# Query heads 0 and 1 projected as a column pair, keys normalised together, attention in twelve steps a group with the compressed branch inside

## The chip, the cores and the metric

One Trainium2 chip, of which the kernel uses one core. The metric is the device time of one launch, in microseconds (us); less is better. The engines are named as in the profile: PE (TensorE, matrix products; PEld is its weight load), DVE (VectorE), ACT (ScalarE), POOL (GpSimd), SP (SyncE, which issues the large loads).

## The reference, cut to what matters

One block over 256 tokens of width 4096: a normalised input is multiplied by `w_in`, parts of the product go to an mLSTM branch and to an attention branch with 16 heads in 4 groups, both are gated, and two more 4096-wide products follow (`w_out`, `ple_gate`). All is in float32. The change touches the projections of queries and the attention branch:

```
u = rmsnorm(x) @ w_in          # split: ..., ns_q (2048), ns_kc, ns_vc, ns_ks, ns_vs, ns_kw, ns_vw, ...
q = rmsnorm(ns_q per head)     # 4 groups of 4 heads, head width 128
p_c = softmax(q @ kcmp + bias) # 15 compressed keys of a group
o_c = p_c @ vcmp
o_s = softmax(q @ ks + bias) @ vs   # "selected" branch; with 256 tokens all blocks are chosen
o_w = softmax(q @ kw + bias) @ vw   # window branch, 256 keys, causal
o   = g0 * o_c + g1 * o_s + g2 * o_w
```

## The kernel before, in words

Every large product is made in three passes over a split of both sides into a rounded float32r part and its remainder (`whi`, `wlo` for weights; `sh`, `sl` for activations), and the products of a 128 x 128 block with 512 columns are the unit of PE's work. Weights are streamed in tiles of two 128-row blocks by 512 columns (`raw`, six buffers). A **unit** of the main loop takes one such tile: it issues the split of the tile three units ahead (`whi` on ACT, then `wlo` on DVE, four buffers each), then the 12 products of its own tile, and then one step from each of three queues of background generators (`urgent`, `fifo`, `third`). All engines run the instructions of this one written order, each in its own queue. An instruction waits for what it reads and for the buffer that it writes; what stands behind it on its engine waits too.

Columns of `w_in` are taken in **wide groups** (one 512-column stretch, 16 units, 192 products) or in **pair groups** (`pair_group`, two stretches at once, with a plan in `PLANS` that names 16 row blocks `kp`). In a pair group a row block is either plain (`C`, 24 products) or mixed (`a`/`c`, 7 sub-products of 3 passes, 21 products, with extra sums of weights on DVE, `sums`). The accumulators of a pair group lie in PSUM as `own` and `oth`: one set in the four `mm` banks, the other in the four `sd` banks (`side(i)`, one buffer each), by `bset`.

The attention of a query group is a generator (`t_nq`). It normalises the queries, transposes them, splits them into `qh` and `ql`, makes the compressed branch (scores of 15 keys, softmax, weights, a transpose, in steps of their own), and then walks over eight score tiles (one head, 128 queries of half t): `scores` into `sd0` (PE), `bias_max` (DVE), `expo` (ACT), `coef` (DVE), `scale` (ACT, one unit later), `trans` into `sd1` (PE), `copy_pt` (DVE), `pv` (PE). A tile of t = 0 has 256 columns (two branches of 128 keys), one of t = 1 has 512. A new step is one turn of the main loop, so a step's PE work stands behind 12 large products.

Lines of the kernel before that are named below: L869, L871 (products of wide groups), L1135 (products of pair groups), L1416 and L1417 (`whi`, `wlo`), L475 (compressed scores), L484 to L488 (their bias, maximum, difference), L490 (their exponential), L493 to L500 (their weights), L505 (copies of `vcmp`), L523 (first pass of scores), L534, L536 (bias, maximum), L541 (exponentials), L547 (second half of `coef`), L558 (transposes of weights), L563 (their copy), L1112 (sums of `own` at the end of an early pair group).

Of the kernel before, what the change touches and what calls it, by code (L numbers as in the profile page):

```python
# [63 lines left out]
PLANS = {g: FULL for g in (-4, -3, -2, 1, 2)}  # L64
PLANS[-5] = SIX
PLANS[-9] = PLANS[-7] = SIX
PLANS[-8] = _plan((0, 1, 2, 3, 4, 5), (7, 9, 11, 13), (6, 8, 10, 12), (14, 15))
# [16 lines left out]
def hymba_block(ctx: ExitStack, tc: tile.TileContext, a, out: bass.AP):  # L84
# [40 lines left out]
    pad = sm_.tile([128, 16], F32, name="pad")  # L125
# [29 lines left out]
    rt = cp.tile([128, 2], F32, name="rt")  # L155
    cw = cp.tile([128, 3], F32, name="cw")
# [49 lines left out]
    def t_rms():  # L206
# [11 lines left out]
        yield  # L218
        rsqrt(rt, ss, D)
# [23 lines left out]
    def evac_u(ps, flag):  # L243
        u = utile([128, 2, 512])
        scaled(u[:, 0], ps[0], 0, True)
        scaled(u[:, 1], ps[1], 1, False)
        done.add(flag)
        return u

    def transposed(u, t):  # L250
        p = side(t, [128, 4, 128])
# [50 lines left out]
    def t_small(st):  # L302
        while "own-9" not in done:
            yield
# [49 lines left out]
    def normed(u):  # L354

        sq = sqtile([128, 8, 128])
        v = u.rearrange("p t (h d) -> p (t h) d", d=128)
        nc.scalar.activation(sq, v, AF.Square)
        yield
        ss = small([128, 8], "ss8")  # L360
        nc.vector.tensor_reduce(ss, sq, axis=AX.X, op=OP.add)
        yield
        nc.scalar.activation(ss, ss, AF.Sqrt, scale=1.0 / HD, bias=epst)
        yield
        nc.vector.reciprocal(ss, ss)
        nc.vector.tensor_tensor(v, v, ss[:, :, None].to_broadcast([128, 8, 128]), op=OP.mult)
        yield

    def t_k(u, br):
        if br == 0:  # L370
            for i, n in enumerate(("kh", "kl")):
                held[n] = wk.tile([128, 4, 2, 256], F32R, tag=f"nat{i}", name=n)
        kh, kl = held["kh"], held["kl"]
        yield from normed(u)
        pp = [transposed(u, 0), transposed(u, 1)]
        yield
        c = cw[:, br + 1:br + 2]
        for t in range(2):
            r = slice(t * 128, (t + 1) * 128)
            nc.scalar.activation(kh[:, :, br, r], pp[t], AF.Copy, scale=c)  # L380
            nc.vector.scalar_tensor_tensor(kl[:, :, br, r], pp[t], c, kh[:, :, br, r], op0=OP.mult, op1=OP.subtract)
        yield
# [9 lines left out]
    def t_cmp2():  # L392
        hs = held["hs"]
        hp = wk.tile([128, 2, 4, 128], F32, tag="qt", name="hp", bufs=2)
        nc.gpsimd.memset(hp, 0.0)
        yield
        pp = [side(2, [128, 2, 60]), side(3, [128, 2, 60])]
# [7 lines left out]
        for h in range(4):  # L405
            for c in range(2):
                nc.vector.tensor_copy(hp[:, c, :, 32 * h:32 * h + NCMP],
                                      pp[1][:, c, :].rearrange("p (g b) -> p g b", b=NCMP))
            if h % 2:
                yield  # L410
# [9 lines left out]
        kn = stile([60, 128])  # L420
        nc.scalar.activation(kn, pk, AF.Square, accum_out=ss[0:60])
        nc.scalar.activation(vcmp, pv, AF.Copy)
        yield
        rsqrt(ss[0:60], ss[0:60], HD)
        kn = stile([60, 128])
        nc.scalar.activation(kn, pk, AF.Copy, scale=ss[0:60, 0:1])
        yield
        p = side(3, [128, 60])
        nc.tensor.transpose(p, kn, idn[0:60, 0:60])
# [7 lines left out]
    def t_evac(ps, flag):  # L437
        held[flag] = evac_u(ps, flag)
        unread.append(flag)
        yield  # L440

    def t_nq(flag, g):

        u = held.pop(flag)
        yield from normed(u)
# [9 lines left out]
        yield  # L455
# [10 lines left out]
        for h in range(2):  # L466
            load_tb(h)
        yield
        while "cmp" not in done:
            yield  # L470

        pc = side(0, [128, 8, NCMP])
        for t in range(2):
            for h in range(4):
                MM(pc[:, 4 * t + h, :], qt[:, h, t * 128:(t + 1) * 128], kct[:, g, :], start=True, stop=True)  # L475
        yield

        bd = sqtile([128, 4, 128])
        nc.gpsimd.memset(bd, 0.0)
        sc = small([128, 8, 32], "sc", 1)  # L480
        nc.gpsimd.memset(sc, 0.0)
        scv = sc[:, :, 0:NCMP]
        for t in range(2):
            nc.vector.tensor_tensor(scv[:, 4 * t:4 * t + 4], pc[:, 4 * t:4 * t + 4],  # L484
                                    biasc[:, 8 - 8 * t:23 - 8 * t, 4 * g:4 * g + 4].rearrange("p c h -> p h c"), op=OP.add)
        m8 = small([128, 8], "mx8")
        nc.vector.tensor_reduce(m8, scv, axis=AX.X, op=OP.max)
        nc.vector.tensor_tensor(scv, scv, m8[:, :, None].to_broadcast([128, 8, NCMP]), op=OP.subtract)  # L488
        yield
        nc.scalar.activation(scv, scv, AF.Exp)  # L490
        yield
# [1081 lines left out]
```

## Time and profile before

| | us |
|---|---|
| median of 3 runs | 2117.85 (2117.15 to 2119.14) |
| profiled execution | 2118.3 |
| its span, first to last instruction | 2116.5 |
| PE busy in the span | 2107.0 |
| DVE busy | 1679.7 |
| ACT busy | 1198.6 |
| POOL busy | 30.3 |

The profiled execution took 2118.3 us, of which the traced instructions span 2116.5. TensorE's granted clock is at its full level in all of the span. Products are pipelined: a 128x512 one is shown with 390 ns, but the next starts earlier, so the cost of one is read from starts and counts, not from its own length.

### The profile page before, as it was taken

Reading aid. Unit: us, or ns where it says so; the run is one execution under the profiler, and the core shown is the slowest. Engines: PE = TensorE matmul, PEld = TensorE weight load, DVE = VectorE, ACT = ScalarE, POOL = GpSimd, SP = SyncE. Lnnn points to the kernel's source line nnn. Section 1 sums busy time; section 2 is a strip of 40 time slices with the busy share of each in tenths; the row PEclk is TensorE's granted clock in tenths of the full one; section 3 lists DMA queues with packets and bytes.
Section 4 is the critical chain, followed back from the end, with each engine's and each line's share of the span. In section 5 each row is a group of like instructions: output and inputs, shape, how many; then the busy total and the mean of one; then the engine's idle time right before and its main releaser. Section 6 shows DMA issues by size and latency. Waiting matters only on the chain.

```text
span 2116.5 us, 26925 instructions
## 1 busy us (share of the span) xinstructions
PE 2107.0 (100%) x9696; PEld 1739.3 (82%) x9696; DVE 1679.7 (79%) x2130; ACT 1198.6 (57%) x1545; POOL 30.3 (1%) x69
## 2 busy tenths in 40 slices
PE   9999999999999999999999999999999999999998
PEld 7888788888888888888888888888888888888887
DVE  6697588666656675859989999988898987888988
ACT  6656455555556555456555565666555555555554
POOL 1000000000000000000000000000000000000000
PEclk9999999999999999999999999999999999999999
DMA  9656866654455455646666667565666665666664
GB/s 354 211 185 206 285 203 216 195 167 159 145 174 159 151 177 168 196 145 200 200 206 209 192 207 229 182 213 180 224 211 216 229 221 169 204 201 224 203 218 145
DMA packets 118374, 422.08 MB, mean 199 GB/s; under 512 B 13714, under 2 KB 14026, under 8 KB 118240
## 3 DMA queue, kind: packets, MB, share of 16 engines
q1 hardware_dynamic: 115568, 413.45, 60.4%
q0 software_dynamic: 2528, 6.89, 1.1%
q8 instruction: 76, 1.25, 0.2%
q14 instruction: 58, 0.48, 0.1%
q10 hardware_dynamic: 144, 0.02, 0.0%
HBM read 416.08 MB, written 4.23 MB: 199 GB/s over the span
## 4 chain that ended last, share of the span: by engine, by line
PE 99%; DMA 0%; DVE 0%; ACT 0%; SPq 0%; issue 0%
PE mm L1135 34%; PE sd L1135 33%; PE mm L869 16%; PE mm L871 8%; PE sd L569 1%; PE sd L976 1%; PE sd L558 1%; PE sd L253 0%; PE sd L773 0%; PE sd L582 0%; PE sd L475 0%; DMA raw<-in_w_in 0%; PE sd L525 0%; PE sd L524 0%; PE sd L523 0%; PE mm L956 0%
## 5 line engine op out<-in xcount | busy, mean ns | idle before, releaser
L1416 ACT ACTIVATE whi<-raw 128x1024 fp32r<-128x1024 f32 x839 | 885.1, 1060 | 732.5 <-PE mm L869 133.8
L1417 DVE TENSOR_TENSOR wlo<-raw,whi 128x1024 fp32r<-128x1024 f32 x839 | 1021.9, 1222 | 343.1 <-ACT whi L1416 327.1
L1135 PE MATMUL sd<-whi,sh 128*128 128x512 f32 x852 | 276.1, 390 | 0.0
L1135 PE MATMUL sd<-wlo,sh 128*128 128x512 f32 x852 | 275.7, 389 | 0.0
L1135 PE MATMUL sd<-whi,sl 128*128 128x512 f32 x852 | 275.6, 389 | 0.0
L1135 PE MATMUL mm<-whi,sh 128*128 128x512 f32 x840 | 272.9, 393 | 0.3 <-ACT mv L200 0.3
L1135 PE MATMUL mm<-whi,sl 128*128 128x512 f32 x840 | 270.0, 389 | 0.0
L1135 PE MATMUL mm<-wlo,sh 128*128 128x512 f32 x840 | 269.9, 389 | 0.0
L869 PE MATMUL mm<-whi,sh 128*128 128x512 f32 x768 | 245.1, 400 | 1.4 <-ACT whi L1416 1.4
L869 PE MATMUL mm<-whi,sl 128*128 128x512 f32 x768 | 237.4, 390 | 0.0
L871 PE MATMUL mm<-wlo,sh 128*128 128x512 f32 x768 | 237.1, 390 | 0.0
L1135 PEld LDWEIGHTS sd<-wlo,sh 128*128 128x128 f32 x852 | 159.9, 188 | 33.2
L1135 PEld LDWEIGHTS sd<-whi,sl 128*128 128x128 f32 x852 | 159.9, 188 | 33.2
L1135 PEld LDWEIGHTS sd<-whi,sh 128*128 128x128 f32 x852 | 159.6, 188 | 33.3 <-issue 0.4
L1135 PEld LDWEIGHTS mm<-whi,sl 128*128 128x128 f32 x840 | 157.7, 188 | 33.1
L1135 PEld LDWEIGHTS mm<-wlo,sh 128*128 128x128 f32 x840 | 157.6, 188 | 33.1 <-DVE wlo L1417 0.2
L1135 PEld LDWEIGHTS mm<-whi,sh 128*128 128x128 f32 x840 | 155.8, 188 | 34.4 <-issue 2.7
L871 PEld LDWEIGHTS mm<-wlo,sh 128*128 128x128 f32 x768 | 144.0, 188 | 31.6 <-DVE wlo L1417 0.8
L869 PEld LDWEIGHTS mm<-whi,sl 128*128 128x128 f32 x768 | 144.2, 188 | 31.0
L869 PEld LDWEIGHTS mm<-whi,sh 128*128 128x128 f32 x768 | 139.6, 189 | 29.1 <-issue 1.9
L1135 PE MATMUL mm<-whi,cb 128*128 128x512 f32 x416 | 134.6, 389 | 0.0
L1135 PE MATMUL sd<-whi,cb 128*128 128x512 f32 x352 | 117.5, 389 | 0.0
(315 smaller groups left out, 1875.2 us busy)
## 6 DMA issues: line engine op xcount, KB each, us to landing
raw<-in_w_gate SPq DMA_DIRECT2D x192, 512.0 KB, 3.6
raw<-in_w_in SPq DMA_DIRECT2D x191, 512.0 KB, 3.5
raw<-in_w_out SPq DMA_DIRECT2D x128, 512.0 KB, 4.0
raw<-in_ple_gate SPq DMA_DIRECT2D x128, 512.0 KB, 3.5
raw<-in_w_early SPq DMA_DIRECT2D x96, 512.0 KB, 3.9
raw<-in_w SPq DMA_DIRECT2D x16, 512.0 KB, 4.3
u<-in_xt SPq DMA_DIRECT2D x16, 256.0 KB, 7.7
xn<-in_x SPq DMA_DIRECT2D x4, 1024.0 KB, 7.1
```

The lines of the kernel that those rows point to most:

```text
L558: nc.tensor.transpose(psd[i][:, b, s, :], sb[i][:, b, s * 128:(s + 1) * 128], idn)
L569: MM(o[t][:, h, :], ptb[i][:, b, s, :], v[:, s, b, g * 128:(g + 1) * 128], start=False, stop=(i == 6 + t and b == 1 and s == t))
L869: MM(box["ps"][t], s[c][:, k, t * 128:(t + 1) * 128], m[:, j, :], start=st, stop=False)
L871: MM(box["ps"][t], sh[c][:, k, t * 128:(t + 1) * 128], lo[:, j, :], start=False, stop=last)
L976: MM(o[64 * kv:64 * kv + 60], xq[l // 8][:, l % 8, 60 * kv:60 * kv + 60], raw[:, j, 256 * kv:256 * kv + 256], start=(l == 0), stop=(l == 31))
L1135: MM(acc.t, s, m, start=acc.i == 0, stop=acc.i == acc.n - 1)
L1416: nc.scalar.activation(hi, r, AF.Copy)
L1417: nc.vector.tensor_sub(lo, r, hi)
```

## The change

The query stretches nq0 and nq1 leave the wide groups and become a pair group, -7, with five mixed row blocks; the early pair groups before it move up by one number (-10, -9, -8). Group -5 takes the plan FULL (seven mixed) in place of SIX. The two key branches are normalised and transposed in one generator (`t_keys`). Queries are no longer scaled before their norm (the epsilon is scaled instead, `epsr`). The normalisation of a query group is a generator of its own in the third queue (`t_query`). In `t_nq` two tiles of t = 0 are joined (four 128-key blocks, 512 columns), so that there are six score tiles, the compressed branch's work is distributed over the first five steps of the tile loop, and `pv` follows a tile four steps later, not three.

```diff
-EARLY = {-9: ("vs", "vw"), -8: ("mv0", "mv1"), -7: ("ks", "kw")}
-ORDER = ["kc", "vc", "small", -9, -8, -7,
-         "nq0", "nq1", "nq2", "nq3", "mq0", "mk0", "mq1", "mk1", "mv2", "mv3"]
+EARLY = {-10: ("vs", "vw"), -9: ("mv0", "mv1"), -8: ("ks", "kw"), -7: ("nq0", "nq1")}
+ORDER = ["kc", "vc", "small", -10, -9, -8, -7,
+         "nq2", "nq3", "mq0", "mk0", "mq1", "mk1", "mv2", "mv3"]
...
-PLANS = {g: FULL for g in (-4, -3, -2, 1, 2)}
-PLANS[-5] = SIX
+PLANS = {g: FULL for g in (-5, -4, -3, -2, 1, 2)}
+PLANS[-7] = _plan((0, 1, 2, 4), (3, 5, 7, 9, 11), (6, 8, 10, 12, 13), (14, 15))
...
+        def cmp_weights():
+            sm = small([128, 8], "sm8")
+            nc.vector.tensor_reduce(sm, scv, axis=AX.X, op=OP.add)
+            nc.vector.reciprocal(sm, sm)
...
+        tiles = [((0, 1), 0), ((0,), 1), ((1,), 1), ((2, 3), 0), ((2,), 1), ((3,), 1)]
...
-        for i in range(11):
+        for i in range(10):
 
             at(scores, i)
+            if i == 0:
+                cmp_scores()
             at(trans, i - 2)
-            if i == 2:
-                for t in range(2):
-                    MM(o[t].rearrange("p h d -> p (h d)"), pct[:, t, :], bd.rearrange("p h d -> p (h d)"),
-                       start=True, stop=False)
-            at(pv, i - 3)
+            if i == 3:
+                cmp_trans()
+            if i == 4:
+                cmp_values()
+            at(pv, i - 4)
             at(bias_max, i)
             at(copy_pt, i - 2)
             at(expo, i)
             at(coef, i)
-            if i < 8:
+            if i < 4:
+                (cmp_max, cmp_exp, cmp_weights, cmp_copy)[i]()
+            if i < 6:
                 behind.append(lambda i=i: scale(i))
             yield
...
-        bset = g % 2
+        bset = (g + (g < -6)) % 2
...
-                evq.extend(("oth-7", "oth-7"))
+                evq.extend(("own-7", "own-7"))
```

Three places in the orders of the engines' queues matter. The first is DVE's queue in the first query group, at the third score tile. Of the kernel before, from one split to the next (`wlo` is the split of a weight tile, `s` the scores with their bias, `mx` their maximum, `pt` the copy of transposed weights, `sm` the sums of exponentials):

```order
L1417 TENSOR_TENSOR wlo_3913<-raw_3735,whi_3912 128x1024
L534 TENSOR_TENSOR s_3943<-sd0_3932,tb_3675 128x512
L536 TENSOR_REDUCE mx2_3945<-s_3943 128x2
L563 COPY pt_3947<-sd1_3936 128x512
L546 RECIPROCAL sm2_3949<-sm2_3949 128x2
L547 TENSOR_TENSOR sm2_3949<-sm2_3949,sg_118 128x2
L1417 TENSOR_TENSOR wlo_3955<-raw_3754,whi_3954 128x1024
```

Of the changed kernel, DVE's queue from one split to the next at step 2 (`sc` holds the compressed scores, `sm8` their sums):

```order
L1471 TENSOR_TENSOR wlo_4172<-raw_3982,whi_4171 128x1024
L570 TENSOR_TENSOR s_4200<-sd0_4191,tb_4073 128x512
L573 TENSOR_REDUCE mx_4202<-s_4200 128x2
L604 COPY pt_4204<-sd1_4195 128x512
L586 RECIPROCAL sm_4206<-sm_4206 128x2
L588 TENSOR_TENSOR sm_4206<-sm_4206,sg_119 128x2
L520 TENSOR_REDUCE sm8_4211<-sc_4095 128x8
L521 RECIPROCAL sm8_4211<-sm8_4211 128x8
L522 TENSOR_TENSOR sm8_4211<-sm8_4211,sg_119 128x8
L524 TENSOR_TENSOR sc_4095<-sc_4095,sm8_4211 128x8x15
L526 TENSOR_TENSOR sc_4095<-sc_4095,mask01_c_101 128x4x15 x2
L1471 TENSOR_TENSOR wlo_4223<-raw_4002,whi_4222 128x1024
```

The weights of the compressed branch (L520 to L526), which before stood between two splits with no score tile beside them, now stand behind a score tile's `coef`. On ACT, at steps 1 and 2 of the changed kernel, the exponential of the compressed scores (L516) and the four copies of `vcmp` (L530) stand between the tile's exponentials and the next `whi`:

```order
L581 ACTIVATE s_4157,sm_4163<-s_4157,mx_4159 128x256 x2
L516 ACTIVATE sc_4095<-sc_4095 128x8x15
L1470 ACTIVATE whi_4171<-raw_3982 128x1024
L592 ACTIVATE s_4157<-s_4157,sm_4163 128x256 x2
L581 ACTIVATE s_4200,sm_4206<-s_4200,mx_4202 128x256 x2
L530 ACTIVATE sq_4168<-vcmp_121 32x128 x4
L1470 ACTIVATE whi_4222<-raw_4002 128x1024
```

In the kernel before these two pieces stood between two `whi` with no tile's exponentials between. The second place is PE's queue at step 3 of the changed kernel, from the last large product of the unit to the first of the next (`sd0` takes the scores, `sd1` the transposes of tile 1, `sd2` the transposes of the compressed weights `sc`):

```order
L916 MATMUL mm1_3884<-wlo_4078,sh6_427 128x512
L560 MATMUL sd0_4242<-k_3299,qh_4062 128x256
L561 MATMUL sd0_4242<-k_3299,ql_4063 128x256
L562 MATMUL sd0_4242<-k_3300,qh_4062 128x256
L560 MATMUL sd0_4242<-k_3299,qh_4062 128x256
L561 MATMUL sd0_4242<-k_3299,ql_4063 128x256
L562 MATMUL sd0_4242<-k_3300,qh_4062 128x256
L599 MATMUL sd1_4249<-idn_81,s_4157 128x128 x4
L535 MATMUL sd2_4254<-idn_81,sc_4095 128x128 x2
L914 MATMUL mm0_3883<-whi_4131,sh6_427 128x512
```

And at step 4 (the products with `pct`, the copy of those transposes, open the output banks):

```order
L916 MATMUL mm1_3884<-wlo_4132,sh6_427 128x512
L560 MATMUL sd0_4294<-k_3299,qh_4062 128x512
L561 MATMUL sd0_4294<-k_3299,ql_4063 128x512
L562 MATMUL sd0_4294<-k_3300,qh_4062 128x512
L599 MATMUL sd1_4298<-idn_81,s_4200 128x128 x4
L545 MATMUL sd2_4303<-sq_4168,pct_4096 128x512
L545 MATMUL sd3_4304<-sq_4168,pct_4096 128x512
L611 MATMUL sd2_4303<-vsw_1744,pt_4204 128x128 x4
L914 MATMUL mm0_3883<-whi_4171,sh7_484 128x512
```

Both pieces stood in units without score tiles, or two units after their input, in the kernel before; now each stands one step behind the DVE work that it reads. The third place is the end of pair group -7 of the changed kernel, on PE (`mm0_3163` to `mm1_3166` are the `own` accumulators, `mm0_3883` and `mm1_3884` the first two of the wide group nq2):

```order
L1189 MATMUL mm1_3165<-wlo_3799,sh7_484 128x512
L1189 MATMUL mm1_3166<-wlo_3799,sh7_484 128x512
L914 MATMUL mm0_3883<-whi_3818,sh0_153 128x512
L914 MATMUL mm1_3884<-whi_3818,sh0_153 128x512
L914 MATMUL mm0_3883<-whi_3818,sl0_154 128x512
L914 MATMUL mm1_3884<-whi_3818,sl0_154 128x512
```

and on DVE, where those accumulators are read:

```order
L1158 TENSOR_TENSOR u_3792<-mm0_3163,u_3792 128x512
L1158 TENSOR_TENSOR u_3792<-mm0_3164,u_3792 128x512
L1158 TENSOR_TENSOR u_3793<-mm1_3165,u_3793 128x512
L1158 TENSOR_TENSOR u_3793<-mm1_3166,u_3793 128x512
L1471 TENSOR_TENSOR wlo_3878<-raw_3772,whi_3877 128x1024
```

A name mm0 or mm1 has two buffers, so the first accumulator of nq2 takes the buffer of `mm0_3163` and the second that of `mm1_3165`. In the kernel before, the last early pair group held its `own` accumulators in the `sd` banks, and the wide group behind it began in `mm` banks.

## Rows read from the trace of the kernel before

**Rows 1.** The page, part 4: shares of the chain that ended last.

```profile
PE 99%; DMA 0%; DVE 0%; ACT 0%; SPq 0%; issue 0%
```

**Rows 2.** Busy time by engine (us, instructions) in a stretch of gate pair groups.

```profile
1025.00:1100.00 75.00, 75.00 (x332) 62.10 (x331) 67.62 (x75) 42.69 (x47) 0.00 (x0) 1.00 0.63 202
```

**Rows 3.** Timeline, DVE, first query group: start, us, engine, line, out<-in [idle before].

```profile
463.94 0.42 DVE L534 TENSOR_TENSOR s<-sd,tb 128x256 f32<-128x256 f32 x1 [1.08 <-PE sd L525]
464.40 0.42 DVE L536 TENSOR_REDUCE mx<-s 128x2 f32<-128x256 f32 x1
...
467.87 0.69 DVE L534 TENSOR_TENSOR s<-sd,tb 128x512 f32<-128x512 f32 x1
468.59 0.69 DVE L536 TENSOR_REDUCE mx<-s 128x2 f32<-128x512 f32 x1
...
470.63 0.16 DVE L547 TENSOR_TENSOR sm<-sm,sg 128x2 f32<-128x2 f32 x1
471.38 1.23 DVE L1417 TENSOR_TENSOR wlo<-raw,whi 128x1024 fp32r<-128x1024 f32 x1 [0.59 <-ACT whi L1416]
472.52 0.42 DVE L534 TENSOR_TENSOR s<-sd,tb 128x256 f32<-128x256 f32 x1
```

**Rows 4.** Timeline, ACT, the same stretch.

```profile
464.86 0.40 ACT L541 ACTIVATE s<-s,mx 128x128 f32<-128x128 f32 x1 [3.59 <-DVE mx L536]
...
465.65 1.04 ACT L1416 ACTIVATE whi<-raw 128x1024 fp32r<-128x1024 f32 x1
...
469.31 0.51 ACT L541 ACTIVATE s<-s,mx 128x256 f32<-128x256 f32 x1 [2.03 <-DVE mx L536]
...
470.31 1.04 ACT L1416 ACTIVATE whi<-raw 128x1024 fp32r<-128x1024 f32 x1
```

**Rows 5.** Timeline, all engines, two score tiles before the group's last.

```profile
495.14 0.69 DVE L536 TENSOR_REDUCE mx<-s 128x2 f32<-128x512 f32 x1
...
495.74 0.68 DVE L563 COPY pt<-sd 128x512 f32<-128x512 f32 x1
...
496.57 0.41 PE L558 MATMUL sd<-idn,s 128*128 128x128 f32 x2
```

**Rows 6.** Timeline, PE, first query group.

```profile
463.74 0.63 PE L869 MATMUL mm<-whi,sh 128*128 128x512 f32 x2
...
474.93 0.39 PE L523 MATMUL sd<-kh,qh 128*128 128x512 f32 x1
...
475.62 0.60 PE L558 MATMUL sd<-idn,s 128*128 128x128 f32 x4
476.05 0.61 PE L569 MATMUL sd<-vsw,pt 128*128 128x128 f32 x4
```

**Rows 7.** Timeline, PE, compressed scores of the first query group.

```profile
447.69 1.85 PE L475 MATMUL sd<-kct,sq 128*128 128x15 f32 x16
449.39 0.72 PE L869 MATMUL mm<-whi,sh 128*128 128x512 f32 x2
```

**Rows 8.** Timeline, DVE, compressed branch of the first query group.

```profile
450.46 0.42 DVE L484 TENSOR_TENSOR sc<-sd,biasc 128x60 f32<-128x60 f32 x2 [0.66 <-POOL sc L481]
...
451.23 0.29 DVE L488 TENSOR_TENSOR sc<-sc,mx 128x120 f32<-128x120 f32 x1
...
457.00 0.27 DVE L493 TENSOR_REDUCE sm<-sc 128x8 f32<-128x120 f32 x1
...
458.07 0.35 DVE L500 TENSOR_TENSOR sc<-sc,mask_c 128x60 f32<-128x60 f32 x2
```

**Rows 9.** Timeline, ACT, compressed branch of the first query group.

```profile
454.42 0.30 ACT L490 ACTIVATE sc<-sc 128x120 f32<-128x120 f32 x1
...
458.46 1.25 ACT L505 ACTIVATE sq<-vcmp 32x128 f32<-32x128 f32 x4
```

**Rows 10.** Timeline, DVE: sums of the last early pair group's own accumulators.

```profile
378.16 2.48 DVE L1112 TENSOR_TENSOR u<-sd,u 128x512 f32<-128x512 f32 x4
```

**Rows 11.** Timeline, PE: first products of the wide group behind it.

```profile
378.89 0.62 PE L869 MATMUL mm<-whi,sh 128*128 128x512 f32 x2
```

More of the change, by code (lines that the diff above doesn't have):

```diff
@@ L218, in t_rms @@
         yield
+        nc.vector.tensor_scalar(epsr, ss, EPS / D, EPS * EPS, op0=OP.mult, op1=OP.add)
         rsqrt(rt, ss, D)
@@ L302, in t_small @@
     def t_small(st):
-        while "own-9" not in done:
+        while "own-10" not in done:
             yield
@@ L435, in hymba_block, with t_evac, t_query @@
     unread = deque()
-    def t_evac(ps, flag):
-        held[flag] = evac_u(ps, flag)
+    def t_evac(ps, flag, plain):
+        held[flag] = evac_u(ps, flag, plain)
         unread.append(flag)
         yield
+    def t_query(flag, g):
+        while g and f"bd{g - 1}" not in done:
+            yield
+        yield from normed([held[flag]], sqtile([128, 8, 128]))
+        done.add(f"query{g}")
     def t_nq(flag, g):
+        while f"query{g}" not in done or "cmp" not in done:
+            yield
         u = held.pop(flag)
-        yield from normed(u)
         pp = [transposed(u, 0), transposed(u, 1)]
@@ L464, in load_tb @@
                                                ap=[[1, 128], [1, 256]]))
-        for h in range(2):
+        for h in range(3):
             load_tb(h)
         yield
[L469 to L473, printed above, removed]
-            for h in range(4):
[L475 to L488, printed above, removed]
@@ new lines, in cmp_trans, with cmp_copy, cmp_values @@
+        def cmp_trans():
+            pp = cm["pp"] = side(2, [128, 2, 128])
+            for t in range(2):
+                nc.tensor.transpose(pp[:, t, :], sc[:, 4 * t:4 * t + 4, :].rearrange("p h c -> p (h c)"), idn)
+        def cmp_copy():
+            nc.vector.tensor_copy(cm["pct"], cm["pp"])
+        o = []
+        def cmp_values():
+            o.extend((side(2, [128, 4, 128]), side(3, [128, 4, 128])))
+            for t in range(2):
+                MM(o[t].rearrange("p h d -> p (h d)"), cm["pct"][:, t, :], cm["bd"].rearrange("p h d -> p (h d)"),
+                   start=True, stop=False)
+            done.add(f"bd{g}")
@@ L536, in bias_max @@
+            mx[i] = small([128, 4], "mx", 3)[:, 0:2 * len(hs)]
             nc.vector.tensor_reduce(mx[i], sb[i], axis=AX.X, op=OP.max, negate=True)
+            if i == 1:
+                load_tb(3)
         def expo(i):
-            sums[i] = small([128, 2], "sm2", 3)
-            for b in range(2):
+            n = 2 * len(tiles[i][0])
+            sums[i] = small([128, 4], "sm", 3)[:, 0:n]
+            for b in range(n):
                 nc.scalar.activation(sb[i][:, b], sb[i][:, b], AF.Exp, bias=mx[i][:, b:b + 1],
```

257 lines of the change are left out of this document (140 added, 117 removed).

## Prediction

> **What bounds the kernel now.** I read first the chain of work that ended last: 99% of it is PE, and every other engine rounds to nothing [rows 1]. So time is gained only by taking work from PE or by closing a wait of PE, and any new wait of PE is paid in full. Second, the price of a product: in a stretch with large products alone, 75.00 us hold 332 of them [rows 2], 0.226 us each, whatever length one is shown with. Third, the stage that the change rewrites. There the reader should follow DVE and ACT through one score tile, because they are linked in a loop: DVE adds the bias (467.87) and takes the maximum (468.59), ACT then makes the exponentials (469.31) and only behind them, in its queue, the next weight split `whi` (470.31), DVE's `wlo` waits for that (471.38, after 0.59 of idling), and the next tile's bias stands behind `wlo` (472.52) [rows 3, 4]. This loop took 4.65 us for a tile of 512 columns (472.52 - 467.87) and 3.93 for one of 256 (467.87 - 463.94). A step of PE with its 12 products takes about as long. Near the group's end PE already waits a little: a transpose starts at 496.57, just 0.15 after the copy that frees its bank ended (495.74 + 0.68) [rows 5]. The stage has no slack left in this loop, only the lead of some microseconds that PE's queue gives at its start.
>
> **What is removed.** Two wide groups are 2 x 192 = 384 products; the pair group -7 has 11 plain and 5 mixed row blocks, 11 x 24 + 5 x 21 = 369. Group -5 gets one more mixed block, 3 products fewer. 18 products x 0.226 = **4.07 us less**. The sums and splits that the mixed blocks add lie on DVE under products: in a stretch of such groups DVE is busy 67.62 of 75.00 and PE is never idle [rows 2], so I cost them at nothing; uncovered they would cost what is over: some 25 instructions of 128x512 at 0.69 [rows 3], 17 us on DVE, of which that stretch has 7 free in every 75, so at most a few us.
>
> **What stays.** Scores, transposes and value products are the same in number. Two steps fewer in a group mean fewer changes between large and small products on PE; no row prices one, I take nothing.
>
> **Attention, step by step.** Prices, all from start to start or to the end of a row: 256-column bias 0.46; 512-column bias 0.72; maximum to first exponential 0.72 (468.59 to 469.31); two exponentials of 256 in 1.00, two of 128 in 0.79, so four in 1.58; `whi` to `wlo` 1.07; `wlo` to next bias 1.14; `coef` ends 0.48 after `whi` starts (470.63 + 0.16 - 470.31) [rows 3, 4]; maximum to copy 0.60, copy 0.68 [rows 5]. A single tile's loop is therefore 0.72 + 0.72 + 1.00 + 1.07 + 1.14 = 4.65, as seen. A joined tile has two biases and four exponentials: 0.92 + 0.72 + 1.58 + 1.07 + 1.14 = 5.43.
>
> The compressed branch adds to it. At step 0 its bias and maximum take 1.06 on DVE (450.46 to 451.23 + 0.29) [rows 8] behind `coef`: 0.48 + 1.06 = 1.54 against the 1.07 that DVE would wait for `whi`, so +0.47. At step 1 its exponential (0.30) and at step 2 the copies of `vcmp` (1.25) [rows 9] stand ahead of `whi` on ACT. The weights at step 2 take 1.42 on DVE (457.00 to 458.07 + 0.35) [rows 8], inside that wait. The loops of steps 0, 1, 2 are thus 5.90, 4.95 and 5.90.
>
> PE's steps: 12 products 2.71; scores 0.69 and transposes 0.43 [rows 6]; compressed scores 1.70 (447.69 to 449.39) [rows 7]. With step 0's first product at 0: scores end at 3.40, DVE starts 0.20 later (463.94 after PE's scores gave way at 463.74) [rows 3, 6]: 3.60. Biases start at 3.60, 9.50, 14.45, 20.35. Without waits PE's steps start at 0, 5.10 (2.71 + 0.69 + 1.70), 8.50, 12.33.
>
> - Step 3 of PE wants to transpose the compressed weights at 12.33 + 2.71 + 0.69 + 0.43 = 16.16. They are ready on DVE at 14.45 + 0.72 + 0.72 + 1.00 + 0.48 + 1.42 = 18.79, on PE 0.15 later: 18.94. **A wait of 2.78.** The tile's own transpose ahead of it waits for the copy of tile 0 (14.45 + 0.72 + 0.60 + 0.68 = 16.45 + 0.15, wanted 15.73), inside the same 2.78.
> - Two transposes, 0.21, then step 4 starts at 19.15 and wants the products with `pct` at 19.15 + 3.83 = 22.98. The copy `pct` stands behind `coef` of step 3: 20.35 + 0.92 + 0.72 + 1.58 + 0.48 + 0.42 (a 256-column instruction) = 24.47, + 0.15 = 24.62. **A wait of 1.64.**
>
> Behind PE's waiting instruction stand all large products of the next unit; nothing can pass. Later steps have no further wait by the same count: PE is late itself by then. **4.42 us a group, 17.7 for four groups.** No row of before shows the joined order, so both ends: if DVE never waited for ACT, its work to the end of `pct` would be some 15 us after 3.60 by the same rows, that is before 22.98 and even before PE's unhindered wish, and the price is 0; the full coupling gives 17.7. I take 17.7, since the rows show the coupling in each step.
>
> **A bank.** Group -7 ends in `mm` banks and the wide group nq2 begins in them. In the kernel before, the four sums took 378.16 to 380.64 [rows 10], so the third ends near 380.04 (pitch 0.60), while the wide group's products began at 378.89 unhindered [rows 11]. In the changed kernel the second of these wants the bank of the third sum: 380.04 + 0.15 - (378.89 + 0.23) = **1.07 us**. Bounds: 0 if the sums come early, 2 if DVE is late.
>
> The keys' generator has 8 plain units of 2.71 before group -7 needs its `sd` banks and uses seven; I cost it at nothing, and at 2 us if it is late.
>
> **Sum** against the profiled execution: 2118.3 - 4.07 + 17.7 + 1.07 = 2133.0. The median of the runs shown is 0.45 below that execution: **2132.5**.
>
> **A rule that speaks the other way.** DVE idles in every tile's loop (0.59 before `wlo`), so it is not saturated [rows 3]; a joined tile's loop is 5.43 where two of 256 take 2 x 3.93 = 7.86, so joining shortens the loops of a group by 4.9, while PE's cover shrinks by two units, 5.4, and compressed work moves in. The Trainium skill (Perfetto Trace Analysis, Optimizing Scalar/DVE Operations) says that grouping into larger operations can help throughput when the engine is saturated, and that where Scalar or Vector are not saturated but make other engines wait, breaking instructions up can let work finish sooner. By its first half the change would hide all of its waits; by its second it goes the wrong way, as my sum has it; this trace bears out the second.
>
> **Rivals.**
> 1. *All hidden (faster).* The lead that PE's queue leaves is larger than my walk says, and `pct` is copied before PE wants it. It decides at one point: `pct` done before 20.2 in my count (step 4's wish without any wait, 12.33 + 3.83 + 0.21 + 3.83), 4.4 earlier. Then only the products count: 2118.3 - 4.07 - 0.45 = 2113.8, and about 2113 if the group's fewer changes on PE give something. For it: PE's present waits in this stage are only tenths. Against: today's tiles come with half the columns every other step, and no compressed work beside them.
> 2. *Tiles alone.* The compressed work fits into DVE's and ACT's idle stretches, and only the tile loops bind: biases at 3.60, 9.03, 13.68, 18.33, 23.76, 28.41, then 33.1; with the next group's square (1.04, as a `whi`) in one of them the fifth copy ends near 34.9, wanted near 33.6 (estimate): 1.3 a group. 2118.3 - 4.07 + 5.3 + 1.07 - 0.45 = 2120.2, no measurable change. Against: the copies of `vcmp` stand ahead of `whi` in one queue.
> 3. *More.* Each wait also costs a restart, and the keys come late: 17.7 + 12 waits of some tenths + 2: 2137.
>
> **How the numbers follow.** About 0.2% (4.2 us) is what a measurement of this kernel can tell from no change. My forecast 67%, spread 2126 to 2136; rival 1 16%, of which somewhat over half falls below 2113.6; rival 2 12%, two thirds of it unchanged; rival 3 5%. Faster 0.10, same 0.14, slower 0.76. The range reaches to 2118, into rival 2, and up to 2137: what is left out is rival 1 and little else. The forecast alone is 2126 to 2136.
>
> **What would show it.** PE has 18 products fewer. Right: in the changed profile PE idles eight times in the attention stage with DVE as releaser, four times before the transposes of `sc` (near 2.8 us) and four before the products with `pct` (near 1.6), and once about 1 us at the start of nq2; PE's idle time in the span is near 19 us more. Wrong: PE without idle time there, or idle at the tile's own transposes alone (rival 2). If `whi` were seen on ACT ahead of a tile's exponentials, or DVE's loops at 4.3 us or less, the walk has failed at its links.

## Result and the profile after

The changed kernel takes **2132.86 us** (median of 6 runs, 2132.45 to 2134.43) where the kernel before takes 2118.25 in the same runs: 1.007 of it, with an interval of 1.0057 to 1.0083. It is slower, by about 14.6 us. Its profiled execution took 2132.45 us, with a span of 2130.7 (before: 2116.5), so the span is 14.2 us longer.

The page, part 1 and part 4, of the changed kernel:

```profile
PE 2108.1 (99%) x9678; PEld 1736.4 (81%) x9678; DVE 1702.6 (80%) x2135; ACT 1206.7 (57%) x1561; POOL 30.7 (1%) x69
...
PE 95%; DVE 2%; ACT 2%; issue 1%; DMA 1%; SPq 0%; ACTq 0%
```

PE has 9678 instructions where it had 9696, 18 fewer. On the chain PE's share has dropped from 99% [rows 1] to 95%, and DVE and ACT, which rounded to nothing, hold 2% each. PE lost work and the kernel got longer, so PE now waits. For what, the view of PE's waits says (line waited at, engine and line waited for: us in total, times, longest):

```profile
PE sd L535 <- DVE sc L526: 6.0, 4, 1.5
PE sd L545 <- DVE pct L538: 3.8, 3, 1.3
...
PE sd L261 <- ACT u L202: 1.2, 2, 0.6
...
PE mm L914 <- DVE u L1158: 0.6, 1, 0.6
```

None of these was in the kernel before. The first row is the transposes of the compressed weights, once in each of four groups; the second is the products with `pct`, in the first three groups only. The last is the bank at the start of nq2. The third row, transposes of the mLSTM's queries and keys (twice), was not foreseen.

In the fourth group something else stands in place of the wait for `pct`. PE's timeline there, and a line of the view by windows behind the wait for `sc` (third-last column: TensorE's granted clock):

```profile
674.66 0.66 PE L535 MATMUL sd<-idn,sc 128*128 128x128 f32 x2 [1.49 <-DVE sc L526]
674.97 1.20 PE L914 MATMUL mm<-whi,sh 128*128 128x512 f32 x2
...
679.23 0.40 PE L560 MATMUL sd<-k,qh 128*128 128x512 f32 x1
...
680.43 1.95 PE L545 MATMUL sd<-sq,pct 128*128 128x512 f32 x4
```
```profile
674.70:678.00 3.30, 3.30 (x9) 2.72 (x10) 2.78 (x5) 1.36 (x4) 0.00 (x0) 0.50 0.18 30
```

The granted clock is 0.50 there, the level of 1.2 GHz. From the two transposes to the next scores PE takes 4.57 us (674.66 to 679.23), where the first group takes 3.00 (513.86 to 516.86). PE comes 1.57 us later to the products with `pct`, and the copy is ready by then. So this stretch cost about what the missing wait would have.

The first query group of the changed kernel, DVE's timeline:

```profile
499.13 0.76 DVE L570 TENSOR_TENSOR s<-sd,tb 128x256 f32<-128x256 f32 x2 [1.52 <-PE sd L562]
...
504.73 0.68 DVE L570 TENSOR_TENSOR s<-sd,tb 128x512 f32<-128x512 f32 x1
...
509.58 0.69 DVE L570 TENSOR_TENSOR s<-sd,tb 128x512 f32<-128x512 f32 x1
...
510.90 0.68 DVE L604 COPY pt<-sd 128x512 f32<-128x512 f32 x1
...
513.49 0.35 DVE L526 TENSOR_TENSOR sc<-sc,mask_c 128x60 f32<-128x60 f32 x2
514.38 1.23 DVE L1471 TENSOR_TENSOR wlo<-raw,whi 128x1024 fp32r<-128x1024 f32 x1 [0.54 <-ACT whi L1470]
515.52 0.75 DVE L570 TENSOR_TENSOR s<-sd,tb 128x256 f32<-128x256 f32 x2
...
519.06 0.42 DVE L538 COPY pct<-sd 128x256 f32<-128x256 f32 x1
```

ACT in the same stretch, between the exponentials of tile 2 and the next split:

```profile
512.02 1.25 ACT L530 ACTIVATE sq<-vcmp 32x128 f32<-32x128 f32 x4
513.29 1.06 ACT L1470 ACTIVATE whi<-raw 128x1024 fp32r<-128x1024 f32 x1
```

And PE, from the first product of step 0's unit to the products with `pct`:

```profile
495.50 0.61 PE L914 MATMUL mm<-whi,sh 128*128 128x512 f32 x2
...
511.73 0.63 PE L599 MATMUL sd<-idn,s 128*128 128x128 f32 x4
513.86 0.41 PE L535 MATMUL sd<-idn,sc 128*128 128x128 f32 x2 [1.50 <-DVE sc L526]
...
517.74 0.63 PE L599 MATMUL sd<-idn,s 128*128 128x128 f32 x4
519.63 1.95 PE L545 MATMUL sd<-sq,pct 128*128 128x512 f32 x4 [1.26 <-DVE pct L538]
```

The loop that the prediction walked is there to see: bias to bias 5.60, 4.85 and 5.94 us, where [rows 3] had 3.93 and 4.65 for single tiles. The copies of `vcmp` stand ahead of `whi`, `wlo` waits for `whi` (0.54), and the next bias stands behind `wlo`. Four transposes take 0.43 [rows 6], so PE lost 513.86 - 511.73 - 0.43 = 1.70 us ahead of `sc` and 519.63 - 517.74 - 0.43 = 1.46 ahead of `pct`, start to start (1.50 and 1.26 by the view, which counts idle time alone).

The bank at the start of nq2, on PE, answering to [rows 11]:

```profile
468.68 0.47 PE L914 MATMUL mm<-whi,sh 128*128 128x512 f32 x1
469.78 0.50 PE L914 MATMUL mm<-whi,sh 128*128 128x512 f32 x1 [0.63 <-DVE u L1158]
```

From start to start 1.10, where one product takes 0.23: 0.87 lost.

### The profile page after: what moved, and what is told of

It is laid out like the page before. It is cut to its first block, busy times and chain, and to the rows that moved or that the text cites. A ratio compares the mean times of both kernels' runs of the same rounds, so it can differ in the third digit from the quotient of the medians.

```text
span 2130.7 us, 26904 instructions
## 1 busy us (share of the span) xinstructions
PE 2108.1 (99%) x9678; PEld 1736.4 (81%) x9678; DVE 1702.6 (80%) x2135; ACT 1206.7 (57%) x1561; POOL 30.7 (1%) x69
## 4 chain that ended last, share of the span: by engine, by line
PE 95%; DVE 2%; ACT 2%; issue 1%; DMA 1%; SPq 0%; ACTq 0%
PE mm L1189 37%; PE sd L1189 33%; PE mm L914 12%; PE mm L916 6%; PE sd L611 1%; ACT s L581 1%; ACT whi L1470 1%; PE sd L1022 1%; DVE wlo L1471 1%; PE sd L261 1%; PE sd L818 0%; DVE mx L573 0%; DVE s L570 0%; PE sd L545 0%; DMA raw<-in_w_in 0%
## 5 line engine op out<-in xcount | busy, mean ns | idle before, releaser
L1189 PE MATMUL mm<-whi,sh 128*128 128x512 f32 x939 | 304.7, 393 | 0.3 <-ACT mv L202 0.3
L1189 PE MATMUL mm<-wlo,sh 128*128 128x512 f32 x939 | 301.4, 389 | 0.1
L1189 PE MATMUL mm<-whi,sl 128*128 128x512 f32 x939 | 301.4, 389 | 0.0
L1189 PEld LDWEIGHTS mm<-wlo,sh 128*128 128x128 f32 x939 | 176.1, 188 | 37.5 <-DVE wlo L1471 0.7
L1189 PEld LDWEIGHTS mm<-whi,sl 128*128 128x128 f32 x939 | 176.3, 188 | 37.1
L914 PE MATMUL mm<-whi,sh 128*128 128x512 f32 x640 | 204.0, 400 | 2.5 <-ACT whi L1470 1.2
L1189 PEld LDWEIGHTS mm<-whi,sh 128*128 128x128 f32 x939 | 174.1, 188 | 38.1 <-issue 2.7
L914 PE MATMUL mm<-whi,sl 128*128 128x512 f32 x640 | 198.2, 391 | 0.0
L916 PE MATMUL mm<-wlo,sh 128*128 128x512 f32 x640 | 197.9, 391 | 0.1
L916 PEld LDWEIGHTS mm<-wlo,sh 128*128 128x128 f32 x640 | 120.3, 188 | 26.4 <-DVE wlo L1471 0.7
L914 PEld LDWEIGHTS mm<-whi,sl 128*128 128x128 f32 x640 | 120.4, 188 | 25.7
L1189 PE MATMUL mm<-whi,cb 128*128 128x512 f32 x432 | 140.4, 389 | 0.0
L914 PEld LDWEIGHTS mm<-whi,sh 128*128 128x128 f32 x640 | 116.7, 189 | 25.0 <-ACT whi L1470 1.6
L1189 PE MATMUL sd<-whi,cb 128*128 128x512 f32 x384 | 127.5, 389 | 0.0
```

Of the source, the lines that this page charges most:

```text
L914: MM(box["ps"][t], s[c][:, k, t * 128:(t + 1) * 128], m[:, j, :], start=st, stop=False)
L916: MM(box["ps"][t], sh[c][:, k, t * 128:(t + 1) * 128], lo[:, j, :], start=False, stop=last)
L1189: MM(acc.t, s, m, start=acc.i == 0, stop=acc.i == acc.n - 1)
```

## The experiments

All kernels are edits of the changed kernel except e8 and e12, which are edits of the kernel before. The kernel before took 2118.6 to 2118.8 us (medians) in these runs; spans are compared with its 2116.5 and with the changed kernel's 2130.7. A time that stands without a number of runs is one execution. Stretches at a granted clock of 0.50, as the one above, stand among the attention steps of e2 (three), e5 (two), e4 and e7 (one each), and e9 (two longer ones, shown there); the other runs have none there.

**e1: a free unit behind each of steps 0 to 3.** The same work, with more of PE's products between the steps.

```diff
             yield
+            if i in (0, 1, 2, 3):
+                yield
```

> The changed kernel with one free unit of the main loop behind each of steps 0 to 3 of the tile loop (16 steps a group, not 12); no work is added or left out. Theory (DVE and ACT need 5 to 6 us for each of the first four steps, PE only 3.4 to 5.1): each free unit gives PE 2.7 us of products while the loop catches up, so the waits for sc and pct vanish, 3.5 us a group: about 2118 us (2116 to 2120). Rival (the waits are a latency of the compressed chain or of restarts, whatever stands between): the time stays within 3 us of 2133.

Measured: 2116.52 us (10 runs), 0.9991 of before (0.9981 to 1.0001), span 2115.2. The waits for `sc` and `pct` are gone from the view of PE's waits, and so are those at the mLSTM's transposes; the bank's 0.6 is still there. So the spacing of the steps carried the loss: 15.5 us of span against the changed kernel. DVE's biases in e1:

```profile
499.55 0.76 DVE L570 TENSOR_TENSOR s<-sd,tb 128x256 f32<-128x256 f32 x2 [1.52 <-PE sd L562]
...
507.50 0.69 DVE L570 TENSOR_TENSOR s<-sd,tb 128x512 f32<-128x512 f32 x1 [0.46 <-PE sd L562]
...
514.12 0.68 DVE L570 TENSOR_TENSOR s<-sd,tb 128x512 f32<-128x512 f32 x1
```

The first loop became 2.35 us longer (7.95 for 5.60, with 0.46 of waiting for PE's scores in it), the second 1.77. PE gained a unit of 2.7 in each, so DVE and ACT didn't stand still: a free unit brings a weight split of its own.

**e2: the compressed branch one step earlier**, in a step ahead of the first tile.

```diff
-        for i in range(10):
+        for i in range(-1, 10):
...
-            if i == 0:
+            if i == -1:
                 cmp_scores()
...
-            if i == 3:
+            if i == 2:
                 cmp_trans()
...
-            if i < 4:
-                (cmp_max, cmp_exp, cmp_weights, cmp_copy)[i]()
+            if i < 3:
+                (cmp_max, cmp_exp, cmp_weights, cmp_copy)[i + 1]()
-            if i < 6:
+            if 0 <= i < 6:
```

> The changed kernel with the compressed branch one step ahead of the score tiles (a step of its own for the compressed scores in front, transposes at step 2; 13 steps a group). Theory (the sum of the loops on DVE and ACT binds, wherever the compressed work stands in them): the wait for pct goes, but the weights, behind step 1's coef, are now wanted earlier by PE too; by the walk 3.2 us before the transposes of sc and 0.5 elsewhere, so no real change, 2133 (2130 to 2136). Rival (the compressed chain is merely one step late against PE): the waits vanish, about 2120.

Measured: 2134.62 us, span 2132.9. The wait for `pct` is gone, the one for `sc` is longer (6.0 before the edit):

```profile
PE sd L535 <- DVE sc L526: 8.5, 4, 2.1
```

Three of these four waits are followed by a stretch at a granted clock of 0.50, where the changed kernel has one. At 1.57 us each the two more are some 3 us of e2's span (an estimate), so the earlier branch alone is about even with the changed kernel, or slightly better. By this run it doesn't matter much where the compressed work stands, as long as it is inside a loop that is longer than PE's step.

**e3: single tiles in the new loop.**

```diff
-        tiles = [((0, 1), 0), ((0,), 1), ((1,), 1), ((2, 3), 0), ((2,), 1), ((3,), 1)]
+        tiles = [((h,), t) for h in range(4) for t in range(2)]
...
-            if 0 <= i < 6:
+            if 0 <= i < 8:
                 f(i)
...
-        for i in range(10):
+        for i in range(12):
...
-            if i < 6:
+            if i < 8:
                 behind.append(lambda i=i: scale(i))
```

> The changed kernel with eight tiles of one head each, as in the kernel before, and the compressed branch inside the loop as changed (14 steps a group). Theory: a tile of 256 columns takes the loop 3.9 us, not 5.4, but PE's step is shorter as well; by the walk 1.5 us before the transposes of sc and 1.5 before pct, 3.0 a group in place of 3.5: about 2131 (2128 to 2133). Rival (the joined tiles make the waits): they vanish, 2118 to 2120.

Measured: 2137.51 us, span 2135.7, 5.0 more than the changed kernel, which I had not expected. The waits for the compressed branch became only a little smaller (5.0 and 3.6), and a new one came, before the tiles' own transposes:

```profile
PE sd L599 <- DVE pt L604: 7.8, 6, 2.1
```

My walk ended at step 4 and left out the later tiles. These waits come twice in each of the first three groups, and not in the fourth, which has no next group whose queries are normalised beside it. With eight tiles the square root of that normalisation (533.13) and the two table loads around it stand between score tiles on ACT, ahead of `whi`. The first load, and the wait that follows:

```profile
531.84 1.28 ACT L376 ACT_TABLE_LOAD   x1
...
537.89 0.41 PE L599 MATMUL sd<-idn,s 128*128 128x128 f32 x2 [1.24 <-DVE pt L604]
```

So what is new in e3 goes with the normalisation (e7 and e9 below take up the same thing), and the run doesn't show that joining helps in this loop. Without its 7.8 us e3's span would be 2127.9, the changed kernel's without its 1.57 at half clock 2129.1 (estimates): about even. No run holds the normalisation back with single tiles in the new loop.

**e4: the compressed branch without its softmax.** On DVE its bias, maximum and weights are gone, on ACT the exponential and the copies of `vcmp`.

```diff
-            if i < 4:
-                (cmp_max, cmp_exp, cmp_weights, cmp_copy)[i]()
+            if i == 0:
+                nc.gpsimd.memset(sc, 0.0)
+            if i == 1:
+                cmp_blocks()
+            if i == 3:
+                cmp_copy()
```

> The changed kernel without the compressed branch's softmax on DVE and ACT: its bias, maximum, exponential, weights and the copies of vcmp are left out (zeros are transposed and multiplied in their place), so the compressed part of the attention is missing from the output; all of PE's instructions stay. Theory (compressed work and joined tiles share the loop): the wait before the transposes of sc goes, pct is still late behind the tile's coef: some 2.0 us a group stay of 3.5, about 2127 (2123 to 2130). Rival A (the compressed branch alone makes the waits): about 2118. Rival B (tiles alone): no change, 2133.

Measured: 2128.27 us, span 2126.5. The wait for `sc` is gone, that for `pct` remains, as expected if the tiles' loops alone are longer than PE's steps:

```profile
PE sd L548 <- DVE pct L541: 5.0, 4, 1.3
```

**e5: one free unit, behind step 2.**

```diff
             yield
+            if i == 2:
+                yield
```

> The changed kernel with one free unit of the main loop behind step 2 alone (13 steps a group). Theory (PE lacks about 3.5 us a group against the loop on DVE and ACT): one free unit gives PE 2.7 us, so the wait for sc goes and some 0.8 us a group stay before pct: about 2122 us (2120 to 2125). Rival (each wait has a cause of its own): the wait for sc goes, that for pct stays at 1.4 us a group or grows: 2125 or more.

Measured: 2133.55 us, span 2131.8. **Wrong by 11.5 us.** DVE, from the bias of tile 2 to that of tile 3:

```profile
511.26 0.68 DVE L570 TENSOR_TENSOR s<-sd,tb 128x512 f32<-128x512 f32 x1
...
516.07 1.23 DVE L1473 TENSOR_TENSOR wlo<-raw,whi 128x1024 fp32r<-128x1024 f32 x1 [0.54 <-ACT whi L1472]
517.82 1.22 DVE L1473 TENSOR_TENSOR wlo<-raw,whi 128x1024 fp32r<-128x1024 f32 x1 [0.52 <-ACT whi L1472]
518.96 0.75 DVE L570 TENSOR_TENSOR s<-sd,tb 128x256 f32<-128x256 f32 x2
```

Two splits stand there, and the loop took 7.70 us instead of 5.94. Of the unit's 2.7 us only 1.0 is a lead. And the wait for `sc`, once removed (0.3 is left), had held PE back for what comes behind it. Two stretches at half clock, one more than in the changed kernel, add to the time. The waits of e5:

```profile
PE sd L545 <- DVE pct L538: 4.8, 4, 1.2
PE sd L560 <- DVE s L570: 2.0, 4, 1.0
PE sd L599 <- DVE pt L604: 1.8, 4, 0.4
```

**e6: free units behind steps 1 and 2, and the bank.** For group -7 the `own` accumulators are put into the `mm` banks in the other order, so that the first two sums free what nq2 takes first.

```diff
             yield
+            if i in (1, 2):
+                yield
...
-            for i, (t, j) in enumerate(((0, 0), (1, 0), (0, 1), (1, 1))):
+            for i, (t, j) in enumerate(((0, 0), (0, 1), (1, 0), (1, 1)) if g == -7 else ((0, 0), (1, 0), (0, 1), (1, 1))):
```

> The changed kernel with one free unit behind steps 1 and 2 each (14 steps a group), and group -7's own accumulators placed so that nq2's first two accumulators take the buffers of the first two sums, not of the first and the third. Theory: 5.4 us of cover for 3.5 us, no wait for sc or pct is left; the wait for the sums at the start of nq2, 0.9 us in the changed kernel, falls to 0.3: about 2116 (2114.5 to 2117.5). Rival (steps 0 and 3 need a free unit too): 2118 or more.

Measured: 2121.84 us (11 runs), 1.0014 of before (1.0005 to 1.0023), span 2120.7. This is above my range, as the rival had it: one wait is left, `pct` with 4.8 in four, and steps 0 and 3 need a unit too (e1, e11). At the bank 0.04 us of waiting is left of 0.63; from start to start the second product comes 0.51 behind the first, not 1.10.

**e7: the changed kernel with the old attention body**: single tiles, compressed steps ahead of them. The frame (pair group -7, keys together, `t_query`) stays new. Its edit, as against the changed kernel, puts the body of `t_nq` of the kernel before in place of the new one, with one line more: the flag that lets `t_query` start, after the products with `pct`.

```diff
-        tiles = [((0, 1), 0), ((0,), 1), ((1,), 1), ((2, 3), 0), ((2,), 1), ((3,), 1)]
+        units = [(h, t) for h in range(4) for t in range(2)]
...
-        for i in range(10):
+        for i in range(11):
...
-            if i == 3:
-                cmp_trans()
-            if i == 4:
-                cmp_values()
-            at(pv, i - 4)
+            if i == 2:
+                for t in range(2):
+                    MM(o[t].rearrange("p h d -> p (h d)"), pct[:, t, :], bd.rearrange("p h d -> p (h d)"),
+                       start=True, stop=False)
+                done.add(f"bd{g}")
+            at(pv, i - 3)
```

> One part alone: the changed kernel's projections, keys, query normalisation and order, with the attention steps of the kernel before (single tiles, the compressed branch in steps of its own ahead of them). Theory (the attention steps alone cost): 18 products less, 4.1 us, and some 2 us of small waits: 2116 (2114.5 to 2118). Rival (the pair group or the keys' generator makes waits too): 2120 or more.

Measured: 2131.77 us (4 runs), 1.0058 of before (1.0043 to 1.0074), span 2130.2. **Wrong by 16 us:** the old loop, which hid nearly everything before, loses almost as much in the new frame as the new loop does. ACT's timeline in the first query group of e7 (L367 squares the queries, L376 is their square root):

```profile
525.60 1.04 ACT L367 ACTIVATE sq<-u 128x1024 f32<-128x1024 f32 x1
526.55 1.04 ACT L1443 ACTIVATE whi<-raw 128x1024 fp32r<-128x1024 f32 x1
...
535.74 1.28 ACT L376 ACT_TABLE_LOAD   x1
537.03 0.48 ACT L376 ACTIVATE ss<-ss,epsr 128x4 f32<-128x4 f32 x2
...
541.12 1.28 ACT L559 ACT_TABLE_LOAD   x1 [2.08 <-DVE mx L554]
```

The next group's normalisation lies beside the score tiles: its square ahead of one `whi`, its square root ahead of another, and a table load on each side of that root. PE waits at the tiles, most of all for biases:

```profile
PE sd L541 <- DVE s L552: 5.3, 5, 1.3
PE sd L576 <- ACT s L559: 3.6, 5, 1.0
PE sd L576 <- DVE pt L581: 2.4, 3, 0.8
```

**e8: the kernel before with the new attention loop alone.** Its `t_nq` has the new body (joined tiles, compressed work inside), all else is old: nq0 and nq1 as wide groups, no `t_query`. Of its edit, the lines that set the order (they are those of the change):

```diff
-        for i in range(11):
+        for i in range(10):
...
-            at(pv, i - 3)
+            if i == 3:
+                cmp_trans()
+            if i == 4:
+                cmp_values()
+            at(pv, i - 4)
...
+            if i < 4:
+                (cmp_max, cmp_exp, cmp_weights, cmp_copy)[i]()
```

> The other part alone: the kernel before, with the changed kernel's attention steps (joined tiles, the compressed branch inside) and all else as it was. Theory: the waits for sc and pct appear here as well, 3.5 us a group: 2118 + 14 = 2132 (2129 to 2135). Rival (they need the changed kernel's surroundings): 2118 to 2122.

Measured: 2134.89 us, span 2133.1, 16.6 more than before. The waits are those of the changed kernel, and here, with no stretch at half clock, `pct` is waited for in all four groups:

```profile
PE sd L517 <- DVE sc L508: 6.0, 4, 1.5
PE sd L527 <- DVE pct L520: 5.0, 4, 1.3
```

**e9: e7 with the next group's normalisation held back until the tile loop's end.**

```diff
             if i == 2:
...
-                done.add(f"bd{g}")
...
             yield
+        done.add(f"bd{g}")
```

> The kernel of e7_old_loop with one edit: the generator that normalises the next group's queries may start only when the tile loop is over (in e7 it starts at the third tile). Theory (in e7 the square, the sum, two table loads and the product of that generator, some 5 us of ACT and DVE a group, stand beside the tiles and make its 11 us of waits): the waits go, 2120 (2118 to 2122). Rival (the pair group's surroundings make them): 2128 or more.

Measured: 2131.64 us (4 runs), 1.0059 of before (1.0045 to 1.0073), span 2129.9. The time is that of e7, and **my figure was wrong by 12 us**, but the time lies elsewhere. All three waits of e7 are gone. In their place PE waits twice, before the third and the fourth group, for the late normalisation itself. PE's timeline at the first of the two, with the granted clock of a stretch ahead of the stop and of one behind it (third-last column of the view by windows):

```profile
634.97 1.05 PE L587 MATMUL sd<-vsw,pt 128*128 128x128 f32 x8
640.96 1.97 PE L261 MATMUL sd<-idn,u 128*128 128x128 f32 x8 [4.93 <-DVE u L380]
642.58 1.20 PE L887 MATMUL mm<-whi,sh 128*128 128x512 f32 x2
643.58 1.05 PE L887 MATMUL mm<-whi,sl 128*128 128x512 f32 x2
```
```profile
630.00:635.00 5.00, 5.00 (x28) 4.19 (x27) 3.07 (x4) 1.84 (x3) 0.00 (x0) 1.00 0.68 212
...
642.50:645.50 3.00, 3.00 (x9) 2.42 (x9) 2.44 (x4) 2.25 (x4) 0.00 (x0) 0.50 0.00 0
```

No large product stands between the last products of one group and the transposes of the next. In the code, a wide group that ends runs the queued steps with no units between (`while len(unread) > 1` in `evac`) until at most one projection is unread; that this loop is what joined them here was read from the code and not tried. Each stop costs 4.93 us, and then some: the granted clock is 0.50 behind it, and a pair of products takes 0.85 to 1.0 from start to start where it took 0.46. So the normalisation beside the tiles is what makes e7's waits, and behind the tiles there was no room for it.

**e10: the same hold in the changed kernel.**

```diff
-            done.add(f"bd{g}")
...
             yield
+        done.add(f"bd{g}")
```

> The changed kernel with that same edit alone (the next group's queries are normalised after the tile loop). Theory (in the changed kernel the waits before sc and pct come at steps 3 and 4, before that generator's work): no real change, 2132 (2130 to 2134). Rival (the generator is the cause there too): 2120 to 2125.

Measured: 2130.58 us, span 2128.8. The waits for `sc` (6.0) and `pct` (5.0, four again) stay; those at the mLSTM's transposes go, and so does the stretch at half clock. These three make 1.2 + 1.57 - 1.2 = 1.6 of the 1.9 us of span that e10 is shorter; why they go isn't shown. In the changed kernel the normalisation is not what binds: its flag is set at step 4 of a loop with six tiles, and its square (523.36 in the first group) comes after both waits.

**e11: e1 with the accumulators of group -7 in e6's order.** 

```diff
             yield
+            if i in (0, 1, 2, 3):
+                yield
...
-            for i, (t, j) in enumerate(((0, 0), (1, 0), (0, 1), (1, 1))):
+            for i, (t, j) in enumerate(((0, 0), (0, 1), (1, 0), (1, 1)) if g == -7 else ((0, 0), (1, 0), (0, 1), (1, 1))):
```

> The kernel of e1_spaced (free units behind steps 0 to 3) with group -7's own accumulators placed as in e6_two_units_bank. Theory: no wait for sc or pct, and 0.6 to 0.9 us less at the start of nq2 than e1's 2116.5: 2115.7 (2114.5 to 2116.8), below both kernels. Rival (that wait only moves): 2116.5.

Measured: **2116.30 us** (11 runs), 0.9988 of before (0.9979 to 0.9997), span 2114.9. It beats the kernel before by 2.5 us and the changed kernel by over 16. Against e1 it gains 0.2 us, too little to tell the theory from its rival: where the bank's 0.63 us of waiting is gone, PE now waits 0.7 for a `whi` at the first mixed products (245.97).

**e12: the kernel before with joined tiles alone**, compressed steps ahead of the loop as before.

```diff
-        units = [(h, t) for h in range(4) for t in range(2)]
+        tiles = [((0, 1), 0), ((0,), 1), ((1,), 1), ((2, 3), 0), ((2,), 1), ((3,), 1)]
...
-        for i in range(11):
+        for i in range(9):
...
```

> The kernel before with joined tiles alone (six tiles, the compressed branch in steps of its own as before, value products three steps behind). Theory (a joined tile's loop is 5.4 us, a single 512 one 4.65, PE's steps 3.4 to 4.6): by the walk PE is late by 2 us a group, at the tiles' own transposes: 2126 (2122 to 2129). Rival (joining by itself costs nothing, the compressed work does): 2118 to 2120.

Measured: 2125.16 us, span 2123.3, 6.8 more than before. The one new wait of size is at a tile's transposes, for ACT's exponentials (2.6 us in seven); most of the rest of the 6.8 is in no wait that the view shows.

## Why the prediction was right, step by step

**What bounds the kernel.** Right: PE. e1 shows it most plainly, with the same work in another spacing and 15.5 us less span.

**18 products fewer, 4.07 us.** The count is in the page. The saving itself is smaller than the term when the waits are gone: e11, without attention waits or bank, has a span 1.6 us below before's. Some 2.5 us went elsewhere, spread over many starts; no run gives them to one cause. The costs put at nothing (the mixed blocks, the keys' generator) are where to look.

**The walk.** Right link by link. Counted from 495.50, biases start at 3.63, 9.23, 14.08 and 20.02, where 3.60, 9.50, 14.45 and 20.35 were worked out. The `sc` transposes start at 18.36 (18.94) and the products with `pct` at 24.13 (24.62).

**The size of the waits, 4.42 a group.** The terms were too large. Against PE's unhindered wish (16.16) the `sc` transposes are 2.20 late, not 2.78. Of these, 1.70 were lost ahead of `sc` and 0.24 ahead of the tile's own transposes, which wait for a copy (510.90 + 0.68, start 511.73; the last score starts at 511.37 and takes 0.12); the other 0.26 are PE's own steps, longer than priced. At step 4, 0.20 were lost ahead of the tile's transposes in the same way and 1.46 ahead of `pct`. Together PE lost 3.60 in such a group. The fourth lost 0.60 ahead of the tile's transposes, 1.69 ahead of `sc`, 1.57 at half clock and 0.07 ahead of `pct`, 3.93. The four make 14.7, where 17.7 stood in the sum. The loop of step 0 was 0.3 shorter than I had it.

**The bank, 1.07.** Measured 0.87 from start to start. Removing the wait (e6: 0.04 left) was worth little in the total: e11 is 0.3 us of span below e1, with a wait of 0.7 elsewhere.

**The sum.** 14.7 + 0.87 - 4.07 = 11.5 where the span grew by 14.2. The rest is 1.2 of unforeseen waits at the mLSTM's transposes and about 1.5 that is not assigned, a remainder such as e1 (1.9) and e11 (2.5) have too. So the close hit is partly luck: waits too large by 3.0 stood in for these, and in the fourth group a stretch at half clock stood in for the wait for `pct`.

**The signs.** Seven of the eight waits of PE for DVE came where they were called for, and so did the one at the bank. PE's idle time in the span (span less busy) is 22.6 us where it was 9.5: 13.1 more, not 19.

**The rivals.** *All hidden* fails at its point: `pct` is copied at 23.98, not before 20.2. It becomes true in direction once PE has the lead (e1, e11), though not in size. *Tiles alone* fails for this kernel, since the compressed work gives the wait for `sc` (e4), but its mechanism is real: without the compressed softmax the kernel is still 9.6 us above before's (e4, with one stretch at half clock), and e12 has 6.8 from joined tiles alone. I had priced it at 5.3. *More* is small: one of the waits did cost a restart (1.57 us, in the fourth group), and no wait at the banks that the keys' generator uses is in the view.

**What the prediction didn't cost.** It left out the normalisation generator beside the tiles. For the changed kernel this did little harm (e10: 1.9 us in all). But the frame and the loop are not independent: the loop alone costs 16.6 us of span (e8), the frame with the old loop 13.7 (e7), both together 14.2. Whoever adds the parts up from separate trials gets twice the loss. In the old loop the next group's normalisation lengthens four of the tile loops. In the new one, with six tiles and the flag set two steps later, only the square falls beside a tile; the square root comes at 532.59, behind the last bias (526.53). With eight tiles in the new loop (e3) the root falls between tiles again, and 7.8 us of waits come back.

**The rule on grouping.** Joining the tiles costs 6.8 us in the old loop (e12). In the new one single tiles are 5.0 slower (e3), but 7.8 us of e3's waits go with the normalisation, so that pair of runs doesn't price the joining. DVE idles before `wlo` in both loops (0.59 [rows 3], 0.54 in the changed kernel), so it is saturated in neither. The Trainium skill (Perfetto Trace Analysis, Optimizing Scalar/DVE Operations) makes saturation the condition under which grouping can help; e12 agrees with its 6.8 us, and e3 speaks neither for it nor against it.

## What to carry to other kernels

When PE is the bound and other engines feed it in steps, add up one step's loop through all queues it passes (here bias, maximum, exponential, weight split, next bias) and compare it with PE's work in the same step; once PE's lead is used up, PE pays what the loop is longer by, step after step. To give such a loop more cover by putting free work between its steps, count what that work brings onto the same queues: a unit of 2.7 us on PE gave a lead of only 1.0 here. And when a wait is closed, look for the next one behind it: e5 closed 5.7 us of waiting and gained nothing. Before a run is taken for the price of one thing, look what else it moved: e3's new waits go with a normalisation that its longer loop took in.

## What was unexpected of the hardware

**A stop can cost more than its length, and its length doesn't tell.** In the changed kernel a wait of 1.50 us in the first group left the granted clock at its full level (2.4 GHz):

```profile
512.00:516.00 4.00, 2.50 (x15) 1.95 (x14) 3.14 (x11) 3.09 (x9) 0.00 (x0) 1.00 0.22 78
```

Behind one of 1.49 us in the fourth group it stood at 0.50 (1.2 GHz), which cost 1.57 us more. In e2 it was at 0.50 behind three of four equal waits of 2.1 us; in e3 it stayed at its full level all through the attention steps, with a wait of 2.1 among them. After e9's 4.93 us of idling it stood at 0.50 from the first transposes on until about 646: eight products took 642.58 to 646.03, 3.45 us, where eight take 1.81 at 0.226 each. What decides it for the shorter waits isn't shown here.

**A square root among exponentials.** In e7 ACT loads a table ahead of the square root and another ahead of the next exponential, 1.28 us each, so a root of 0.48 us takes 3.0 of ACT inside a loop that is 4.65 long. The Trainium skill (ScalarE activation tables: per-element evaluation and per-set limits, What a function is on this engine) says that functions of different sets are one load of 1283 ns apart; the trace agrees, with 1.28.
